# A decoder block on one core: two fetches at other times, and another order of the FFN's steps

## The chip, the cores and the metric

The kernel runs on one core of a Trainium2 chip, in one launch. The metric is the device time of that core in microseconds (us); shorter is better. Engines are named as the profile names them: PE multiplies matrices (PEld is its weight load), DVE and ACT work on vectors, POOL does very little here, SP only issues DMAs. Each engine works through its own instructions in the order of the program and waits for others by semaphores; the same holds for the queue of DMA issues on SP (SPq) and on ACT (ACTq).

## The reference

One layer of a decoder on 256 positions of width 2048, in float32. What matters here, cut down:

```python
a = rmsnorm(h, norm_mix_pre)
proj = a @ w_in                      # 17408 columns, split below
q_a, k_a, v_a, q_r, f_r, i_r, g_r, gate_a, gate_r = split_columns(proj)
attn  = dilated_window_attention(...)          # 8 heads, three groups of keys
r_out = hgrn2_chunked(...) * silu(g_r)         # gated recurrence, normalised
y = sigmoid(gate_a) * (attn @ w_attn_branch) + sigmoid(gate_r) * (r_out @ w_hgrn_branch)
h = h + rmsnorm(y @ w_mix_out, norm_mix_post)

a = rmsnorm(h, norm_ffn_pre)
gt, up = split(a @ w_ffn_gate_up)              # 2 x 5632 columns
ff = (silu(gt) * up) @ w_ffn_down
h = h + rmsnorm(ff, norm_ffn_post)
```

## The kernel before

Every weight is read once from DRAM into a `raw` tile. ACT rounds it to a shorter format (`hi`, or `w` in the profile), DVE subtracts that from the weight (`lo`, or `wl`), and PE makes three products for each pair of operands, high by high, high by low, low by high. A matmul takes 128 rows by 512 columns.

**Items.** The whole layer is a list of items that are run in order by the loop at the end. Two kinds are of interest. A *chunk* (in the middle of the layer: keys, queries, gates, branches) is 512 KB of weights; two chunks share a `raw` tile. A *step* (FFN gate and up, down product, mixing) is 1 MB: two rows of 128 by two groups of 512 columns. Before item i is multiplied, `prepare(i)` splits item i+2 (`AHEAD` is 2), fetches the presums of item i+4, and loads up to item i+5. There are three `raw` tiles, three `w` tiles and three `wl` tiles.

**Plain steps and steps by seven.** An order such as `GATE_UP4` lists pairs (m, kind): m is the pair of input rows, kind is 0 for a plain step of eight products in three parts (24 matmuls), and 1 or 2 for a step by seven, a Strassen-like scheme of seven products (21 matmuls). A step by seven multiplies sums of weights, so its split is longer. With kind 1 the sums are made on DVE in the split itself (`sum`, L432, L438, L439), then rounded by ACT (L437, L440, and L443 for the plain parts `dh`) and subtracted on DVE (L445, L447). With kind 2 the sums were made earlier by `weight_sums`, lie in DRAM as `presum`, and are fetched as `s` (L424 to L428 split them). The input sums that PE needs for it (`h7[m]`) come from `pair_sums`, a generator which runs a piece at a time in `lanes[1]`; lanes advance twice in a step.

**The FFN.** There are eleven blocks of 2 x 512 columns, eight steps each. Block 0 is plain; blocks 1 to 10 take the order `GATE_UP4`. Within a block the steps are counted from 0. Blocks use the two pools of four PSUM banks (`acc` and `aux`) in turn: the four plain sums of a block lie in one pool, and the three sums that only steps by seven write (`p5`, `p6`, `p7`) in the other, which is free again when the block before has been evacuated (`evac_ffn`, L1333). After step 1 of a block (`turn=1`) `turn_act` transposes the result of the block before on PE (L1302) into two banks of that other pool, ACT copies them out (L1303), and they go to DRAM (`acts`). So two of the four banks are held when step 2 begins with `p6`, `p5`, `p7`, in this order; `p7` needs the first that ACT has emptied. In the order of the program the split of step 3 stands before `turn_act`, since `prepare(1)` runs ahead of it.

**The start of the FFN's block 1.** `begin_wides` runs whatever is left in the lanes before block 1, with `flush(lanes[1])`: at that point the sums for m = 0 and 1 are made, those for m = 2 half way, those for m = 3 not begun.

**The down product.** It takes the activations back from DRAM: `fetch_act` issues `act<-acts` on SP, `prep_act` splits them (L572 on ACT, L576 on DVE) inside the split of a down step. The first two activations are asked for by a hook that the last FFN block runs after a step:

```python
wides[-3].post = lambda c: fetch_act(c // 2 - 2) if c in (4, 6) else None
```

The split of the first down step is in `prepare(6)` of that block. The first down block puts its plain sums in the same pool as the last FFN block.

**The gates.** The sigmoid gates of both branches were computed early and lie in DRAM (`waits`). Six of them (512 KB each) are fetched back by `fetch_gates`, all before the first of the 16 chunks that compute the last two gates; those chunks are followed by 16 chunks of the recurrent branch (`evac_rec_branch`, L1092, uses the first four gates) and 16 of the attention branch (L1102 uses the other two). All the while, `weight_sums` reads weights for the presums (`pre`, L299), adds them on DVE four chunks later (L307 to L311) and stores them.

Of the kernel before, what the change touches and what calls it, by code (L numbers as in the profile page):

```python
# [20 lines left out]
P = 128  # L21
# [19 lines left out]
    [(2, 0), (3, 0), (4, 0), (0, 1), (5, 0), (6, 0), (1, 1), (7, 0)],  # L41
    [(2, 0), (3, 0), (0, 1), (4, 0), (1, 1), (5, 0), (6, 0), (7, 0)],
]
GATE_UP4 = [(4, 0), (5, 0), (0, 2), (6, 0), (1, 1), (2, 2), (3, 1), (7, 0)]
PLACE = (0, 2, 1, 3)
DOWN = [[(m, m in by7) for m in range(KF // 2)] for by7 in (range(4, 20, 3), range(3, 19, 3))]

# [52 lines left out]
def tile_hybrid_block(ctx: ExitStack, tc: tile.TileContext, t, out):  # L100
# [13 lines left out]
    def nm(s):  # L114
        serial[0] += 1
        return f"{s}_{serial[0]}"

    def rslot(s):
        return rpool.tile([P, 1024], F32R, tag="r", bufs=16, name=nm(s))

    def hslot(s):
        return hpool.tile([P, 2, 512], F32, tag="h", bufs=4, name=nm(s))
# [77 lines left out]
    def fslot(s):  # L200
        return fp[0].tile([P, 1024], F32, tag="f", bufs=N_F, name=nm(s))
# [13 lines left out]
    blocks, chunks, wides, steps = [], [], [], []  # L215
    items_pre = {}
# [26 lines left out]
    def add_wide_block(*args, **kw):  # L243
        b = Wide(*args, **kw)
        wides.append(b)
        for i in range(len(b.order)):
            n = len(steps)
            slots.append(lambda n=n: load_wide(n))
            items.append((steps, n, len(slots) - 1))
            steps.append([b, i, None, None])  # L250
# [394 lines left out]
    evacs, turns, lanes, queue = deque(), deque(), [deque(), deque()], deque()  # L645
# [3 lines left out]
    def advance(q):  # L649
        if q:  # L650
            try:
                next(q[0])
            except StopIteration:
                q.popleft()
                return

    def flush(q):
        while q:
            advance(q)
# [192 lines left out]
    def nslot(s):  # L852
        return fslot(s).rearrange("p (b c) -> p b c", b=2)

    def fetch(dst, key, rows, **sizes):
        nc.sync.dma_start(dst, waits[key].rearrange(rows, **sizes))
# [3 lines left out]
            vN[half, g] = nslot("v")  # L860
            fetch(vN[half, g], ("v", g, half), "(j two) c -> j two c", two=2)

    def fetch_gates():
        for j in range(4):
            gates["r", j] = nslot("gate")
            fetch(gates["r", j], ("r", j), "(b p) c -> p b c", p=P)
        for j in range(2):
            gates["a", j] = hslot("gate")
            fetch(gates["a", j], ("a", j), "(b p) c -> p b c", p=P)

    qkT, vN = {}, {}

# [200 lines left out]
    gates = {}  # L1073
# [217 lines left out]
    act_t, h7 = [], {}  # L1291
# [19 lines left out]
    def fetch_act(upto):  # L1311
        while len(act_in) <= min(upto, 2 * len(act_t) - 1, KF // 2 - 1):
            x = rslot("act").bitcast(F32)
            nc.sync.dma_start(x, act_t[len(act_in) % (KF // 4)])
            act_in.append(x.rearrange("p (k t) -> p k t", k=4))
# [132 lines left out]
    def start_attention(half):  # L1448
        def go():
            queue.extend(attention(half, h) for h in range(4))  # L1450
        return go
# [5 lines left out]
    def begin_wides():  # L1457
        flush(lanes[0])
        flush(evacs)
        flush(lanes[1])  # L1460

    def more_y(c):
        if c == 3:
# [33 lines left out]
    for half in range(2):  # L1497
        for g in range(3):
            c = 1024 * g + 512 * half
            add_wide(w_in, KD, COL_Q + c, xT, evac_rope(("q", half, g), 0))  # L1500
            if g == 2:
                items_pre[len(chunks)] = lambda half=half: fetch_values(half)
            add_wide(w_in, KD, COL_K + c, xT, evac_rope(("k", half, g), 2,
                     start_attention(half) if g == 2 else None))
    items_pre[len(chunks)] = fetch_gates
    for j in range(2, 4):
        add("N", w_in, KD, COL_GA + 512 * j, xT, evac_gate(("a", j)))
    for j in range(4):
# [17 lines left out]
    for j in range(1, 11):  # L1526
        add_wide_block(w, (512 * j, FF + 512 * j), GATE_UP4, lambda k: hT[0](k),
                       lambda m: h7[m], evac_ffn, j % 2 == 0,
# [3 lines left out]
                       lambda m: a7[m], evac_down, j % 2 == 0, prep=prep_act,  # L1532
                       pre=begin_down if j == 0 else None, turn=3 if j == 0 else None)

    wides[-3].post = lambda c: fetch_act(c // 2 - 2) if c in (4, 6) else None
    back.append(
        weight_sums([n for n, (b, i, *_) in enumerate(steps) if b.order[i][1] == 2])
    )
# [13 lines left out]
    for i in range(len(items)):  # L1552
        kind, n, _ = items[i]
        b, c = kind[n][:2]
# [98 lines left out]
```

## Time and profile before

| | us |
|---|---|
| median of 3 runs | 1719.29 (1718.66 to 1719.31) |
| the profiled execution | 1719.58 |
| its span, first to last instruction | 1717.8 |
| PE busy | 1693.9 |
| DVE busy | 1438.2 |
| ACT busy | 915.8 |

The profiled execution is 0.29 us over the median. In lists of instructions the first column is the start (us from the first instruction), the second the time in us, then engine, line, operation, output and inputs, shapes and count; in brackets the idle time just before it on its engine and what ended it. A matmul shows about 0.39 us there, since it is pipelined; the next one starts much sooner.

### The profile page before, as it was taken

Reading aid. Unit: us, or ns where it says so; the run is one execution under the profiler, and the core shown is the slowest. Engines: PE = TensorE matmul, PEld = TensorE weight load, DVE = VectorE, ACT = ScalarE, POOL = GpSimd, SP = SyncE. Lnnn points to the kernel's source line nnn. Section 1 sums busy time; section 2 is a strip of 40 time slices with the busy share of each in tenths; the row PEclk is TensorE's granted clock in tenths of the full one; section 3 lists DMA queues with packets and bytes.
Section 4 is the critical chain, followed back from the end, with each engine's and each line's share of the span. In section 5 each row is a group of like instructions: output and inputs, shape, how many; then the busy total and the mean of one; then the engine's idle time right before and its main releaser. Section 6 shows DMA issues by size and latency. Waiting matters only on the chain.

```text
span 1717.8 us, 21815 instructions
## 1 busy us (share of the span) xinstructions
PE 1693.9 (99%) x8309; PEld 1422.9 (83%) x8309; DVE 1438.2 (84%) x1654; ACT 915.8 (53%) x1031; POOL 8.7 (1%) x17
## 2 busy tenths in 40 slices
PE   9999999999999999999999999999999999899997
PEld 7888888888888888888888877888888888688886
DVE  6998888867898998875568878988888888798998
ACT  6655555544434334445445556555555555565663
POOL 0000000000000000000000010000000000000000
PEclk9999999999999999999999999999999999999999
DMA  8567666678877776788457646777777777777773
GB/s 288 196 222 258 233 232 225 218 239 300 270 245 254 268 241 233 267 309 291 149 172 276 213 149 223 266 256 255 246 245 245 247 254 255 245 256 265 242 252 128
DMA packets 228905, 413.49 MB, mean 241 GB/s; under 512 B 12816, under 2 KB 79552, under 8 KB 226240
## 3 DMA queue, kind: packets, MB, share of 16 engines
q1 hardware_dynamic: 218544, 373.93, 64.7%
q10 hardware_dynamic: 10192, 38.15, 5.9%
q8 instruction: 65, 1.06, 0.2%
q14 instruction: 40, 0.33, 0.1%
q0 software_dynamic: 64, 0.02, 0.0%
HBM read 376.92 MB, written 35.13 MB: 240 GB/s over the span
## 4 chain that ended last, share of the span: by engine, by line
PE 91%; DVE 4%; DMA 2%; ACT 2%; issue 1%; SPq 0%; DVEq 0%; ACTq 0%
PE acc L137 57%; PE aux L137 32%; DMA pre<-in_w_ffn_gate_up 1%; DVE wl L418 1%; ACT w L416 1%; DMA s<-presum 0%; DMA gate<-waits 0%; DMA act<-acts 0%; PE aux L608 0%; PE aux L930 0%; DVE w L363 0%; PE aux L1302 0%; DVE fz L1429 0%; DVE dl L447 0%; PE acc L1302 0%
## 5 line engine op out<-in xcount | busy, mean ns | idle before, releaser
L137 PE MATMUL acc<-xT,w 128*128 128x256 f32 (+1 forms) x2048 | 367.1, 338 | 0.2 <-DVE w L363 0.2
L418 DVE TENSOR_TENSOR wl<-raw,w 128x2048 fp32r<-128x2048 f32 (+1 forms) x140 | 304.4, 2183 | 69.8 <-ACT w L416 68.0
L137 PEld LDWEIGHTS acc<-xT,w 128*128 128x128 f32 x2048 | 311.4, 188 | 44.9 <-DVE w L363 1.0
L362 ACT ACTIVATE w<-raw 128x1024 fp32r<-128x1024 f32 x176 | 185.9, 1058 | 245.9 <-PE acc L137 182.9
L416 ACT ACTIVATE w<-raw 128x2048 fp32r<-128x2048 f32 (+1 forms) x140 | 254.3, 1826 | 105.1 <-PE acc L137 36.2
L363 DVE TENSOR_TENSOR w<-raw,w 128x1024 fp32r<-128x1024 f32 x176 | 214.9, 1222 | 98.6 <-ACT w L362 98.1
L137 PE MATMUL acc<-w,xT 128*128 128x512 f32 x578 | 169.5, 392 | 2.3 <-DVE w L363 2.3
L437 ACT ACTIVATE w<-sum 128x1024 fp32r<-128x1024 f32 x57 | 60.5, 1062 | 179.8 <-DVE sum L432 172.6
L137 PE MATMUL acc<-w,hT 128*128 128x512 f32 x472 | 152.9, 392 | 0.5 <-DVE hT L619 0.5
L445 DVE TENSOR_TENSOR wl<-sum,w 128x1024 fp32r<-128x1024 f32 x114 | 137.2, 1221 | 13.0 <-ACT w L437 13.0
L137 PEld LDWEIGHTS acc<-w,xT 128*128 128x128 f32 x578 | 108.1, 188 | 24.7 <-DVE w L363 2.6
L137 PE MATMUL aux<-w,hT 128*128 128x512 f32 x360 | 115.7, 389 | 0.0
L447 DVE TENSOR_TENSOR dl<-raw,dh 128x1536 fp32r<-128x1536 f32 x57 | 100.2, 1757 | 14.4 <-ACT dh L443 13.1
L137 PE MATMUL aux<-w,xT 128*128 128x512 f32 x344 | 109.8, 389 | 0.0
L137 PEld LDWEIGHTS acc<-w,hT 128*128 128x128 f32 x472 | 88.4, 188 | 19.4 <-DVE hT L619 0.9
L137 PE MATMUL acc<-wl,hT 128*128 128x512 f32 x236 | 91.9, 389 | 0.0
L137 PE MATMUL acc<-w,a 128*128 128x512 f32 x268 | 84.9, 394 | 6.6 <-DVE e L1333 6.6
L443 ACT ACTIVATE dh<-raw 128x1536 fp32r<-128x1536 f32 x57 | 84.1, 1476 | 8.0 <-PE aux L137 4.4
L137 PE MATMUL aux<-w,a 128*128 128x512 f32 x268 | 83.6, 389 | 0.0
L137 PE MATMUL acc<-w,so 128*128 128x512 f32 x240 | 81.1, 391 | 1.2 <-ACT act L1303 1.2
L137 PEld LDWEIGHTS aux<-w,hT 128*128 128x128 f32 x360 | 67.6, 188 | 14.1
L137 PEld LDWEIGHTS aux<-w,xT 128*128 128x128 f32 x344 | 64.6, 188 | 13.3
(295 smaller groups left out, 2984.3 us busy)
## 6 DMA issues: line engine op xcount, KB each, us to landing
raw<-in_w_in SPq DMA_DIRECT2D x270, 512.0 KB, 4.8
raw<-in_w_ffn_gate_up SPq DMA_DIRECT2D x156, 512.0 KB, 4.8
raw<-in_w_ffn_down SPq DMA_DIRECT2D x88, 512.0 KB, 5.3
pre<-in_w_ffn_gate_up SPq DMA_DIRECT2D x40, 512.0 KB, 6.7
presum<-pre ACTq DMA_DIRECT2D x20, 1024.0 KB, 4.7
s<-presum SPq DMA_DIRECT2D x40, 512.0 KB, 7.0
raw<-in_w_mix_out SPq DMA_DIRECT2D x32, 512.0 KB, 4.9
act<-acts SPq DMA_DIRECT2D x22, 512.0 KB, 6.4
```

The lines of the kernel that those rows point to most:

```text
L137: nc.tensor.matmul(ps, lhsT, rhs, start=start, stop=stop, skip_group_check=True)
L362: nc.scalar.activation(wh, raw, AF.Copy)
L363: nc.vector.tensor_sub(wl, raw, wh.bitcast(F32))
L416: nc.scalar.activation(hi[:, c], raw[:, c], AF.Copy)
L418: nc.vector.tensor_sub(lo[:, c], raw[:, c], hi[:, c].bitcast(F32))
L437: nc.scalar.activation(hi[:, :1024], s[:, :1024], AF.Copy)
L443: nc.scalar.activation(dhi, d, AF.Copy)
L445: nc.vector.tensor_sub(lo[:, c], s[:, c], hi[:, c].bitcast(F32))
L447: nc.vector.tensor_sub(dlo, d, dhi.bitcast(F32))
```

## The change

Four edits. In `GATE_UP4` the fourth and fifth step change places: the steps by seven stood at places 2, 4, 5 and 6, and stand now at 2, 3, 5 and 6. `fetch_gates` is split into six fetches, one before each second chunk from the twelfth on. `begin_wides` no longer runs all sums in `lanes[1]`, but only until those of m = 1 are there; the others go on in the lanes. And the first two activations of the down product are asked for after steps 1 and 3 of the last FFN block, not after 4 and 6.

```diff
-GATE_UP4 = [(4, 0), (5, 0), (0, 2), (6, 0), (1, 1), (2, 2), (3, 1), (7, 0)]
+GATE_UP4 = [(4, 0), (5, 0), (0, 2), (1, 1), (6, 0), (2, 2), (3, 1), (7, 0)]
...
-    def fetch_gates():
-        for j in range(4):
-            gates["r", j] = nslot("gate")
-            fetch(gates["r", j], ("r", j), "(b p) c -> p b c", p=P)
-        for j in range(2):
-            gates["a", j] = hslot("gate")
-            fetch(gates["a", j], ("a", j), "(b p) c -> p b c", p=P)
+    def fetch_gate(key, slot):
+        def go():
+            gates[key] = slot("gate")
+            fetch(gates[key], key, "(b p) c -> p b c", p=P)
+        return go
...
     def begin_wides():
         flush(lanes[0])
         flush(evacs)
-        flush(lanes[1])
+        while 1 not in h7:
+            advance(lanes[1])
...
-    items_pre[len(chunks)] = fetch_gates
+    for j in range(6):
+        key, slot = (("r", j), nslot) if j < 4 else (("a", j - 4), hslot)
+        items_pre[len(chunks) + 12 + 2 * j] = fetch_gate(key, slot)
...
-    wides[-3].post = lambda c: fetch_act(c // 2 - 2) if c in (4, 6) else None
+    wides[-3].post = lambda c: fetch_act(c // 2) if c in (1, 3) else None
```

## The prediction

> **What bounds the kernel now.** The page first: how much of the span PE leaves unused.
>
> ```profile
> span 1717.8 us, 21815 instructions
> ...
> PE 1693.9 (99%) x8309; PEld 1422.9 (83%) x8309; DVE 1438.2 (84%) x1654; ACT 915.8 (53%) x1031; POOL 8.7 (1%) x17
> ```
>
> PE is the bound, and no edit removes a matmul. All that can move is its idle 23.9 us, and what is added to it. So next the waits of PE (us in total, times, longest):
>
> ```profile
> PE acc L137 <- DVE e L1333: 6.6, 1, 6.6
> PE acc L137 <- DVE w L363: 2.5, 2, 2.3
> PE acc L137 <- ACT act L1303: 1.2, 1, 1.2
> PE aux L137 <- DVE dl L447: 1.1, 1, 1.1
> ```
>
> These four lines are what the edits can touch: the first is at the start of the down product, the second among the gate chunks, the other two in FFN block 1. FFN blocks 2 to 10 have no wait of PE: there an edit of the order can only keep the time or add to it.
>
> **Edit 1, the activations.** Here are, from the instructions in order of time, the end of the last FFN block and the start of the down product, then two pieces of the chain that ended last, and one stretch of time (its length, PE, PEld, DVE, ACT and POOL busy, PE's granted clock, DMA share, GB/s).
>
> ```profile
> 1424.91 2.48 DVE L1333 TENSOR_TENSOR e<-aux,e 128x512 f32<-128x512 f32 x4
> ...
> 1448.15 8.74 SPq L285 DMA_DIRECT2D raw<-in_w_ffn_down  x4
> 1456.94 1.94 SPq L1314 DMA_DIRECT2D act<-acts  x1
> 1463.39 0.63 ACT L572 ACTIVATE a<-act 128x512 fp32r<-128x512 f32 x1 [7.40 <-DMA act<-acts]
> 1467.46 0.39 PE L137 MATMUL acc<-w,hT 128*128 128x512 f32 x1
> 1473.67 2.48 DVE L1333 TENSOR_TENSOR e<-acc,e 128x512 f32<-128x512 f32 x4
> 1474.50 0.77 PE L137 MATMUL acc<-w,a 128*128 128x512 f32 x1 [6.65 <-DVE e L1333]
> ```
>
> ```profile
> 1426.16 10.88 PE acc L137 x48
> 1474.50 23.69 PE acc L137 x96
> ```
>
> ```profile
> 1467.80:1500.00 32.20, 25.55 (x110) 21.10 (x110) 26.50 (x31) 16.61 (x17) 0.00 (x0) 0.89 0.74 250
> ```
>
> The fetch stood on SP behind two steps' weight loads, was issued at 1456.94 and had landed at 1463.39. ACT stood still 7.40 us in front of it, and behind L572 stood on ACT and DVE the splits of two down steps, the gathering of the sevens, and L1333, which empties the banks that the down product needs. PE's last matmul began at 1467.46, the next at 1474.50. At 10.88 / 48 = 0.227 us a matmul, that is 7.04 - 0.23 = 6.8 us lost.
>
> Then the chain: 96 matmuls took 23.69 us, at 0.227 they take 21.77, so 1.9 us more went at a lower clock (0.89 on the mean of that stretch). Together 8.7 us. The Trainium skill, "TensorE: Matmul & The Clock Gate", section "What's actually happening", says that after an idle window of about 3.4 us the array runs at half rate until it has been busy about as long. By that the loss would be some 1.7 us (an estimate from the page), the sum 8.5; the row, 1.9, is taken, and it agrees.
>
> What is late next, once the fetch is early? It now follows the load of step 6 on SP. That load waits for the split of step 3 to free its `raw` tile, which I put at about 1441 below, so the data lie there near 1448, some 8 us before the split of the first down step can start (1456). The second fetch comes before the load of the second down step. Neither moves behind a wait of its own: their two `act` slots were freed by the split of step 2 and by step 0 of this block. On SP the loads of steps 7 and of the first two down steps now stand behind a 512 KB fetch each, half a step's bytes.
>
> The new last link is L1333. In a regular block it starts 1.25 us before the next block's first matmul (1424.91 against 1426.16), and its first quarter (0.62 us) frees the first bank. The down block needs that one at once, because it takes the same pool, and the second bank six matmuls later (1.36 us). That cover holds by 0.6 us. Two L576 (0.7 us each) are new on DVE there against a regular block; the first falls into DVE's old idle time, the second while ACT rounds the weights. So I take the full 8.7; the ends are 0 (the fetch is hidden nowhere) and 8.7.
>
> **Edit 2, the gates.** The instructions, one piece of the chain, two stretches, and the lists for the tiles `pre` and `gate`:
>
> ```profile
> 760.39 3.96 SPq L856 DMA_DIRECT2D gate<-waits  x6
> 779.63 0.48 PE L137 MATMUL acc<-w,xT 128*128 128x512 f32 x1
> 779.79 0.69 DVE L307 TENSOR_TENSOR pre<-pre 128x512 f32<-128x512 f32 x1 [5.36 <-DMA pre<-in_w_ffn_gate_up]
> 782.40 2.79 PE L137 MATMUL acc<-w,xT 128*128 128x512 f32 x11 [2.29 <-DVE w L363]
> ```
>
> ```profile
> 768.40 11.31 DMA pre<-in_w_ffn_gate_up
> ```
>
> ```profile
> 760.00:785.00 25.00, 22.71 (x108) 18.81 (x107) 16.13 (x26) 8.73 (x11) 0.00 (x0) 1.00 0.92 319
> ...
> 805.00:825.00 20.00, 20.00 (x106) 17.18 (x105) 9.81 (x13) 12.31 (x15) 0.00 (x0) 1.00 0.65 212
> ```
>
> ```profile
> L299 SPq DMA_DIRECT2D pre<-in_w_ffn_gate_up x40: 367/469/1460, 357.6 to 792.8; - x40
> ...
> DMA to landing us min/median/max: 3.8/6.0/11.3
> ```
>
> ```profile
> L1092 DVE TENSOR_TENSOR part<-acc,gate x8: 683/684/686, 828.3 to 870.8; 128x512 f32<-128x512 f32 x8
> ```
>
> Six gates, 3 MB, go out at 760 in a stretch whose DMA share is 0.92. The weights for a presum behind them take 11.31 us to land (median 6.0). DVE stands 5.36 us in front of them with a split (L363) queued behind, and PE waits for that split: 782.40 - 779.63 - 0.23 = 2.5 us, and 0.1 more in the next 11 matmuls. At the median, 6.0 us, the weights land 5.3 us earlier, which is all of DVE's wait. So 2.6 us go; the ends are 0 and 2.6.
>
> What the moved fetches meet: the twelfth chunk is near 800, the last `pre` load went out at 792.8, and the DMA share there is 0.65. One gate on every second chunk (5.4 us of PE) adds 512 KB / 5.4 us, about 97 GB/s, to 212: 309, below the 319 shown. The first gate is used at 828.3, over 20 us after its fetch. Their slots were held by attention and the recurrence, which are further on by then; behind each fetch on SP stands one pair of weight loads, three pairs deep. I cost them at nothing.
>
> **Edit 3, the order, in blocks 2 to 10.** Rows of block 10, before:
>
> ```profile
> 1433.74 2.29 DVE L418 TENSOR_TENSOR wl<-raw,w 128x2048 fp32r<-128x2048 f32 x1
> ...
> 1437.52 1.09 ACT L1303 ACTIVATE act<-aux 128x512 f32<-128x512 f32 x2 [3.91 <-PE aux L1302]
> 1438.90 0.62 PE L137 MATMUL aux<-w,so 128*128 128x512 f32 x2
> 1439.97 1.05 ACT L440 ACTIVATE w<-sum 128x1024 fp32r<-128x1024 f32 x1
> 1440.92 1.47 ACT L443 ACTIVATE dh<-raw 128x1536 fp32r<-128x1536 f32 x1
> 1442.30 2.00 ACT L424 ACTIVATE w<-s 128x1024 fp32r<-128x1024 f32 x2
> 1448.04 1.22 DVE L432 TENSOR_TENSOR sum<-raw 128x1024 f32<-128x1024 f32 x1
> 1450.75 1.06 ACT L440 ACTIVATE w<-sum 128x1024 fp32r<-128x1024 f32 x1 [0.33 <-DVE sum L439]
> ```
>
> Before, step 3 is plain: its rounding on ACT needs nothing from DVE and is done when ACT reaches L1303 (it idles 3.91 us there, for PE). After, step 3 is a step by seven, and on ACT L437, L440 and L443 stand ahead of L1303, L440 waiting for DVE's sums. DVE comes to that split at 1433.74. From L432 to L440 takes 1450.75 - 1448.04 = 2.71, from L440 to L443 0.95, from there to the next instruction of ACT 1.38: L1303 starts at 1433.74 + 5.04 = 1438.78, not 1437.52. PE wants the emptied bank for `p7` at the second matmul of the 1438.90 row, 1439.13. Block 1 shows when it gets one, and edit 4 needs the same rows:
>
> ```profile
> 1060.68 0.40 PE L137 MATMUL acc<-w,so 128*128 128x512 f32 x1
> 1061.67 1.06 ACT L1303 ACTIVATE act<-acc 128x512 f32<-128x512 f32 x2
> 1062.30 0.50 PE L137 MATMUL acc<-w,so 128*128 128x512 f32 x1 [1.22 <-ACT act L1303]
> 1082.34 0.50 PE L137 MATMUL aux<-dl,hT 128*128 128x512 f32 x1 [1.14 <-DVE dl L447]
> ```
>
> ```profile
> 1050.00:1092.00 42.00, 39.64 (x178) 32.21 (x177) 39.81 (x42) 23.91 (x21) 0.00 (x0) 1.00 0.66 226
> ```
>
> There PE resumed 0.63 us after L1303's start. So `p7` gets its bank at 1439.41, 0.28 us late, in each of nine blocks. A wait costs a little more than it shows: 1062.30 - 1060.68 - 0.23 = 1.39 for the 1.22. I take 0.35 a block, 3.2 us in all. The ends are 0 (the margin is a few tenths of a sum of five durations) and 0.7 a block, 6.3.
>
> The gain that edit 3 could bring is that a third neighbouring step by seven no longer has to wait for the `dh`/`dl` tiles of the first; but PE waits for no split in these blocks, so it is worth nothing there. The split of step 3 ends on DVE near 1440.7, 1.6 us before PE wants it (1442.3); the later ones keep 2 us or more. Its `raw` tile is held until then and not until 1436, so the load of step 6 goes out nearly 5 us later, at 1441, for a split that starts at about 1448.5, with 6 us to land: covered.
>
> **Edit 4, the sums in two parts, with edit 3 in block 1.** DVE is busy 39.81 of 42 us here: it is the bound, and PE waited twice, 1.22 and 1.14 (1.4 and 1.3 with the restart). The flush held the split of step 2 back behind the sums of m = 2 and 3; now they come later, but all before steps 5 and 6. Nothing is taken off DVE. The wait at step 6 shrinks; that at `p7` grows, because L1303 now stands behind a step by seven there too. DVE reaches that split at about 1058.3 (the two products of block 0, the split of step 2 and half the sums of m = 2 come first); 5.04 + 0.63 later is 1064.0, 1.7 us after the 1062.30 of before. PE then comes to that place in step 6 at about 1082.7, where it resumed at 1082.34, and DVE is done with that split by then. 0.4 us is within what such a sum can tell: I take 0; the ends are a gain of 2.7 (both waits) and a loss of 1.7.
>
> **Sum.** 1719.58 - 8.7 - 2.6 + 3.2 + 0 = 1711.5 for the profiled execution; the median of the runs is 0.29 lower: 1711.2. This kernel tells 0.2% (3.4 us) from no change.
>
> **Rivals.**
>
> *No wait for `p7`* (0.17): L1303 comes 0.3 us sooner than summed. For it: the margin is that thin. Against: all five durations are rows of these blocks. Then 1711.2 - 3.2 = 1708.0.
>
> *The down product still starts late* (0.14): L1333 or the two splits ahead of it end after PE, because its banks are those of the block before. Against: the 0.6 us of cover. With 2 to 4 us of it left, and part of the slow clock, 1713 to 1715. A rule of the Trainium skill would lead there too: "DMA: Bandwidth & Descriptors", section "Anatomy of one DMA", says that a DMA's semaphore wait is waited out on the issuing sequencer, so a fetch without a free slot would hold the weight loads behind it. The trace agrees (the fetch at 1456.94 came out right behind two such loads).
>
> *Slower* (0.04): ACT's detour through DVE's sums costs far more, because DVE starts step 3's sums later than its split of step 3 now (weights landing late behind a `raw` tile held longer). Each 1 us of that is 9 us of PE. To be 0.2% slower it takes 11.3 + 3.4 = 14.7 over nine blocks, 1.63 a block, so DVE 1.3 us later than 1433.74. Nothing shows that: ACT and DVE had the same bytes there in time. Then 1723 and more.
>
> *The early fetches do nothing* (0.05): the gates merely delay other loads, or the activations land as late. Each alone leaves 1714 or 1719.9.
>
> **Chances.** The forecast 0.60. Faster by over 0.2% (below 1715.9): 0.60 + 0.17 + 0.12 and a little of the last, 0.90; within 0.2% 0.06; slower 0.04. The range from the first rival (1708.0) to the late start (1714.8) leaves out about 2 in 10.
>
> **What would show it.** After: PE's wait for L1333 gone, the clock 1.00 at the start of the down product, no wait of ACT for `act`; no wait of L307 or L363 near 780; new waits of PE on L1303, ten of them, some 0.1 to 0.4 us each and one near 2.8 in block 1; no wait for L447. Wrong would be: waits of PE for L1303 over 0.7 us each, or DVE's L1333 ending after PE's last matmul of block 10.

## The result

The changed kernel takes 1711.36 us (1711.0 to 1712.65) for 1718.84 (1717.51 to 1719.31) before: a ratio of 0.9958, 95% interval 0.9944 to 0.9973, which is 7.2 us (the medians are 7.5 apart). The forecast was 1711.2, 8.1 less than the 1719.29 that it started from. Its profiled execution took 1711.36 us, 8.2 less than the profiled one of before. On its page, the lines for the span and PE:

```profile
span 1709.5 us, 21818 instructions
...
PE 1692.8 (99%) x8309; PEld 1420.4 (83%) x8309; DVE 1440.1 (84%) x1654; ACT 915.6 (54%) x1031; POOL 8.7 (1%) x17
```

PE is idle for 16.7 us now, 23.9 before. Its waits in the changed kernel (us, times, longest):

```profile
PE acc L137 <- ACT act L1301: 2.8, 1, 2.8
...
PE acc L137 <- DVE hT L619: 0.5, 1, 0.5
```

The list of the weight load's waits (PEld) has two more lines for ACT's copies, ten waits in all, where before it had one of 1.7 us:

```profile
PEld acc L137 <- ACT act L1301: 5.5, 5, 3.3
PEld aux L137 <- ACT act L1301: 2.8, 5, 0.6
```

Lines after the edited functions are two lower here: L1301 is L1303 of before, L1331 is L1333. The waits for L1333 (6.6), L363 (2.5) and L447 (1.1) are gone. One has grown: PE in block 1 waits 2.8 us for ACT's copies, 1.2 before.

**The start of the down product**, in the changed kernel, in order of time:

```profile
1441.61 0.75 SPq L1312 DMA_DIRECT2D act<-acts  x1
1449.36 0.41 SPq L1312 DMA_DIRECT2D act<-acts  x1
1456.11 0.61 ACT L572 ACTIVATE a<-act 128x512 fp32r<-128x512 f32 x1
1466.95 2.48 DVE L1331 TENSOR_TENSOR e<-acc,e 128x512 f32<-128x512 f32 x4
1467.80 0.39 PE L137 MATMUL acc<-w,hT 128*128 128x512 f32 x1
1468.03 0.39 PE L137 MATMUL acc<-w,a 128*128 128x512 f32 x1
```

The chain there, and the stretch (length, PE, PEld, DVE, ACT, POOL busy, PE's granted clock, DMA share, GB/s):

```profile
1462.07 27.88 PE acc L137 x123
```

```profile
1463.00:1495.00 32.00, 32.00 (x147) 26.55 (x147) 26.02 (x30) 20.22 (x20) 0.00 (x0) 1.00 0.79 265
```

The fetch leaves 15 us earlier, ACT no longer waits before L572, and PE runs through at a clock of 1.00: 27.88 / 123 = 0.227 us a matmul across the boundary. The block's last matmul (1467.80) and the down product's first (1468.03) are 0.23 us apart.

**The gates.** A line of the list of the tile `pre` (how long its loads took to land) and one of `gate`, DVE's first sum of the presum that was late before, and a stretch:

```profile
DMA to landing us min/median/max: 4.1/6.1/10.1
```

```profile
L856 SPq DMA_DIRECT2D gate<-waits x6: 413/464/995, 796.7 to 828.6; - x6
```

```profile
773.30 0.68 DVE L307 TENSOR_TENSOR pre<-pre 128x512 f32<-128x512 f32 x1
```

```profile
800.00:810.00 10.00, 10.00 (x58) 8.68 (x57) 5.33 (x5) 5.21 (x6) 0.00 (x0) 1.00 0.99 340
```

L307 does not wait there any more. Right behind the first of the moved fetches, from 800 to 810, the DMA share is 0.99, and PE is still fully busy.

**Blocks 2 to 10.** ACT's copies in blocks 2 and 10, before and after, give the length of a block:

```profile
1103.97 1.09 ACT L1303 ACTIVATE act<-aux 128x512 f32<-128x512 f32 x2 [3.91 <-PE aux L1302]
```

```profile
1101.78 1.06 ACT L1301 ACTIVATE act<-aux 128x512 f32<-128x512 f32 x2
```

And block 10 after, around the copies:

```profile
1433.66 1.22 DVE L432 TENSOR_TENSOR sum<-raw 128x1024 f32<-128x1024 f32 x1
...
1436.37 1.06 ACT L440 ACTIVATE w<-sum 128x1024 fp32r<-128x1024 f32 x1 [0.30 <-DVE sum L439]
1437.33 1.47 ACT L443 ACTIVATE dh<-raw 128x1536 fp32r<-128x1536 f32 x1
1438.71 1.06 ACT L1301 ACTIVATE act<-aux 128x512 f32<-128x512 f32 x2
1438.82 1.01 PE L137 MATMUL aux<-w,so 128*128 128x512 f32 x2
1439.68 0.40 PE L137 MATMUL aux<-wl,so 128*128 128x512 f32 x1
1449.25 1.23 DVE L432 TENSOR_TENSOR sum<-raw 128x1024 f32<-128x1024 f32 x1 [0.89 <-DMA raw<-in_w_ffn_gate_up]
```

Eight blocks from 1103.97 to 1437.52 were 41.69 us each; from 1101.78 to 1438.71 they are 42.12. L1301 starts 5.05 us after L432, as summed (5.04). The two matmuls at 1438.82 take 1.01 us for the 0.62 of before: the second is `p7`'s first, held for its bank. It starts 0.3 us late. No wait of PE is listed for it, because most of that time hides inside the 0.39 us for which a pipelined matmul is shown. The nine short waits stand in the weight load's list above (with the one of block 1), and what they cost, 3.8 us, is read from the length of a block.

**The account**, by matmuls and transposes of PE that both traces have (start before, start after). Where the stretch with the gates begins (757.86, 756.82) the changed execution is already 1.0 us ahead, though the two kernels are the same up to there. At the first matmul of the mixing product that waits for L1102 (915.11, 911.48) it is 3.6 ahead, so the gates bring 2.6. At the transposes ahead of the copies in block 2 (1103.34, 1099.86) it is 3.5 ahead: block 1 costs 0.15. At those of block 10 (1436.88, 1436.80) it is 0.1 ahead, and one more wait for `p7` follows: blocks 2 to 10 cost 3.8. The last matmul (1708.13, 1699.90) is 8.2 ahead, so the start of the down product brings 8.6. These add up to the 8.2 by which the two profiled executions differ.

### The profile page after: what moved, and what is told of

It reads as the page before. It is cut to its first block, busy times and chain, and to the rows that moved or that the text cites. A ratio compares the mean times of both kernels' runs of the same rounds, so it can differ in the third digit from the quotient of the medians.

```text
span 1709.5 us, 21818 instructions
## 1 busy us (share of the span) xinstructions
PE 1692.8 (99%) x8309; PEld 1420.4 (83%) x8309; DVE 1440.1 (84%) x1654; ACT 915.6 (54%) x1031; POOL 8.7 (1%) x17
## 4 chain that ended last, share of the span: by engine, by line
PE 84%; DVE 7%; issue 5%; ACT 3%; DMA 1%; SPq 0%; DVEq 0%; ACTq 0%
PE acc L137 55%; PE aux L137 28%; ACT w L416 2%; DVE e L1331 1%; DVE wl L418 1%; DVE wl L425 1%; DVE e L1337 1%; DVE sum L432 1%; ACT w L424 1%; DMA pre<-in_w_ffn_gate_up 1%; DVE sum L439 0%; DVE sum L438 0%; PE aux L928 0%; ACT act L1301 0%; PE aux L608 0%
## 5 line engine op out<-in xcount | busy, mean ns | idle before, releaser
L418 DVE TENSOR_TENSOR wl<-raw,w 128x2048 fp32r<-128x2048 f32 (+1 forms) x140 | 305.3, 2184 | 88.0 <-ACT w L416 86.0
L363 DVE TENSOR_TENSOR w<-raw,w 128x1024 fp32r<-128x1024 f32 x176 | 214.9, 1222 | 102.5 <-ACT w L362 101.9
L447 DVE TENSOR_TENSOR dl<-raw,dh 128x1536 fp32r<-128x1536 f32 x57 | 100.1, 1757 | 6.8 <-ACT dh L443 3.4
L137 PE MATMUL aux<-w,so 128*128 128x512 f32 x222 | 76.2, 394 | 0.6
```

What stands on the lines that cost most here:

```text
L137: nc.tensor.matmul(ps, lhsT, rhs, start=start, stop=stop, skip_group_check=True)
L363: nc.vector.tensor_sub(wl, raw, wh.bitcast(F32))
L418: nc.vector.tensor_sub(lo[:, c], raw[:, c], hi[:, c].bitcast(F32))
L447: nc.vector.tensor_sub(dlo, d, dhi.bitcast(F32))
```

## The experiments

All ratios are against the kernel before, timed beside the run.

**Edit 1 alone.**

```diff
-    wides[-3].post = lambda c: fetch_act(c // 2 - 2) if c in (4, 6) else None
+    wides[-3].post = lambda c: fetch_act(c // 2) if c in (1, 3) else None
```

> The kernel before with edit 1 alone (both activations asked for after steps 1 and 3 of the last FFN block). Theory: PE's wait at the start of the down product (6.6 us) and the slow clock behind it (1.9 us) both go, 8.7 us less than before, and no wait of PE on L1333 is left. Rival (the down product starts late anyway, because L1333 or the two down splits are the next link): 4 to 6 us less, with a wait of 2 to 4 us left in front of the first down matmul.

1711.63 us for 1719.70; ratio 0.9950 (0.9938 to 0.9963), 8.1 us less. No wait for L1333 is left:

```profile
PE acc L137 <- DVE w L363: 2.4, 1, 2.4
PE aux L137 <- DVE dl L447: 1.3, 1, 1.3
PE acc L137 <- ACT act L1303: 1.3, 1, 1.3
```

The theory holds, and edit 1 alone gives as much as all four together: the other three sum to about nothing. In this execution the clock falls behind the wait of 2.4 us near 780, which costs 1.6 us more (last section).

**Edit 2 alone** (its last lines; `fetch_gates` is split as above).

```diff
...
-    items_pre[len(chunks)] = fetch_gates
+    for j in range(6):
+        key, slot = (("r", j), nslot) if j < 4 else (("a", j - 4), hslot)
+        items_pre[len(chunks) + 12 + 2 * j] = fetch_gate(key, slot)
```

> The kernel before with edit 2 alone (the gates fetched one by one from the twelfth chunk on). Theory: the weights for the presum land within about 6 to 7 us, DVE does not wait for them, PE's wait near 780 goes: 2.6 us less. Rival (the gates delay other loads where they are now): 0 to 2 us less, with a new wait of PE on L363 between 795 and 845.

1717.36 for 1719.70; ratio 0.9984 (0.9975 to 0.9993), 2.3 us less. The wait near 780 is gone, and no wait of PE appears between 780 and 845. The theory holds. PE's wait at the down product is 7.6 us in its trace (6.6 before), so part of the gain is given back there in this run.

**Edit 3 alone.**

```diff
-GATE_UP4 = [(4, 0), (5, 0), (0, 2), (6, 0), (1, 1), (2, 2), (3, 1), (7, 0)]
+GATE_UP4 = [(4, 0), (5, 0), (0, 2), (1, 1), (6, 0), (2, 2), (3, 1), (7, 0)]
```

> The kernel before with edit 3 alone (steps by seven at places 2, 3, 5, 6, all first sums still made ahead of block 1). Theory (ACT's copies of the transposed result stand behind the sums of step 3): blocks 2 to 10 last 42.1 us instead of 41.7, 3.8 us more; in block 1 DVE reaches step 3's sums at about 1061.8, so the bank for p7 comes at about 1067.5, a wait of some 6.4 us for 1.2 before, and after a wait this long the clock is low for a while (up to 1.9 us more); the wait at the down product shrinks by about 1 us: 6 to 9 us slower than before. Rival (the swap costs nothing, the blocks last longer after the change for another reason): within 1.5 us of before, blocks of 41.7 us.

1729.26 for 1719.70; ratio 1.0053 (1.0040 to 1.0065), 9.6 us more. Its waits of PE, and a stretch behind the one in block 1:

```profile
PE acc L137 <- ACT act L1303: 6.3, 1, 6.3
PE acc L137 <- DVE e L1333: 5.7, 1, 5.7
PE acc L137 <- DVE w L363: 2.9, 1, 2.9
```

```profile
1069.40:1073.00 3.60, 3.60 (x9) 2.88 (x10) 2.00 (x2) 2.98 (x3) 0.00 (x0) 0.53 0.91 320
```

The wait of 6.3 us was expected at 6.4, the smaller wait at the down product at 1 us less (5.7 for 6.6). The clock is 0.53 in the stretch behind the wait in block 1. Blocks 2 to 10 last 42.13 us (ACT's copies in blocks 2 and 10 at 1112.45 and 1449.51). The total is 0.6 over the top of what was expected: behind the wait for L363 (2.9 us here) the clock is low as well (0.61 from 782 to 785), which it was not in the profile of before. The rival falls: this edit costs time by itself.

**Edit 4 alone.**

```diff
-        flush(lanes[1])
+        while 1 not in h7:
+            advance(lanes[1])
```

> The kernel before with edit 4 alone (the sums of m = 2 and 3 left in the lanes). Theory: ACT's copies in block 1 no longer stand behind the sums, so PE's wait for p7 (1.2 us) goes; DVE is the bound of block 1 and is done with the split of step 6 at about 1080.3 to 1081, so a wait of 0.7 to 1.4 us stays there: 1.3 to 1.9 us less than before. Rival (as the prediction had it for edits 3 and 4 together, the wait only moves): within 0.5 us of before.

1717.60 for 1719.70; ratio 0.9987 (0.9978 to 0.9996), 2.1 us less. The wait for ACT's copies is gone and the one at step 6 is smaller:

```profile
PE aux L137 <- DVE dl L447: 0.8, 1, 0.8
```

That is the theory's place, and a little more than its size (1.3 to 1.9); part of the last tenths may be other waits of that execution (L363, 2.0 for 2.3).

**All but edit 3.**

```diff
-GATE_UP4 = [(4, 0), (5, 0), (0, 2), (1, 1), (6, 0), (2, 2), (3, 1), (7, 0)]
+GATE_UP4 = [(4, 0), (5, 0), (0, 2), (6, 0), (1, 1), (2, 2), (3, 1), (7, 0)]
```

> The changed kernel with edit 3 taken back (edits 1, 2 and 4 alone). Theory: blocks 2 to 10 last 41.7 us again, 3.8 us less than with all four edits, and in block 1 the wait for p7 (2.8 us) gives way to a wait of 0.8 us for the split of step 6, as in the run with edit 4 alone: 5 to 6 us less than with all four, 12.5 to 14.5 less than before. Rival (the order earns something at the ends of blocks or at the start of the down product that the sums do not show): no more than 3 us less than with all four, and a wait of PE near 1455 to 1465 that all four do not have.

1705.43 for 1719.35; ratio 0.9916 (0.9903 to 0.9930), 13.9 us less, and 5.9 less than all four edits. In its trace ACT's copies stand at 1098.21 and 1431.76 in blocks 2 and 10, 41.69 us a block; the only wait of PE over 0.5 us from block 1 of the FFN to the end of the down product is that of 0.8 us for step 6 of block 1. This is the fastest order of the steps found here, and it is the old one.

**All four, p7 asked for later.** The same matmuls in another order:

```diff
             prod("p5", sums(0), t, at[1], last)
+            if by7 == 2:
+                prod((1, 1), act_of(1, 1), t, at[3])
             prod("p7", sums(2), t, at[0], last)
-            prod((1, 1), act_of(1, 1), t, at[3])
+            if by7 != 2:
+                prod((1, 1), act_of(1, 1), t, at[3])
```

> The changed kernel, all four edits, with the three matmuls of p7 moved behind the three of the plain sum (1, 1) in the steps by seven whose sums come from DRAM; the same matmuls, p7's bank is asked for 0.68 us later. Theory (blocks 2 to 10 last 0.42 us longer because p7 waits for the bank that ACT empties): those blocks last 41.7 us again and block 1's wait falls from 2.8 to 2.1 us: 4.5 us less than with all four edits, about 12 less than before. Rival (neighbouring steps by seven slow PE or ACT in some other way, or the weights come later): blocks of 42.1 us, at most 0.7 us less.

1708.62 (1706.60 to 1710.28) for 1719.35; ratio 0.9934 (0.9921 to 0.9946). ACT's copies in blocks 2 and 10, and block 1's wait:

```profile
1103.23 1.06 ACT L1304 ACTIVATE act<-aux 128x512 f32<-128x512 f32 x2
...
1436.77 1.06 ACT L1304 ACTIVATE act<-aux 128x512 f32<-128x512 f32 x2
```

```profile
1060.81 0.50 PE L137 MATMUL acc<-w,so 128*128 128x512 f32 x1 [2.13 <-ACT act L1304]
```

```profile
1061.00:1064.00 3.00, 3.00 (x9) 2.37 (x9) 2.93 (x7) 2.40 (x3) 0.00 (x0) 0.59 0.78 251
```

A block lasts 41.69 us again, though ACT's copies still stand behind step 3's sums. That shows that the 0.42 us a block are `p7`'s wait for its bank and nothing else of the new order. The gain on the changed kernel is 2.7 us, not the 4.5 expected: behind the wait of 2.1 us the clock is at 0.59 in this execution.

**The gates in one burst, later** (its last lines; `fetch_gates` is whole again).

```diff
...
-    for j in range(6):
-        key, slot = (("r", j), nslot) if j < 4 else (("a", j - 4), hslot)
-        items_pre[len(chunks) + 12 + 2 * j] = fetch_gate(key, slot)
+    items_pre[len(chunks) + 12] = fetch_gates
```

> The changed kernel with all six gate fetches issued together, ahead of the twelfth chunk (3 MB at about 800 us, when the last weights for a presum are under way or landed). Theory (the gates hurt only by standing in front of the weights that DVE waits for, not by coming together): within 1 us of the changed kernel, no wait of PE on L363. Rival (the burst delays the weights of the chunks wherever it stands): 1.5 to 4 us more than the changed kernel, with a wait of PE between 805 and 825.

1713.40 for 1719.35; ratio 0.9963 (0.9950 to 0.9975). That is 2.0 us more than the changed kernel by the medians, which the theory had not (0.9 us by the two ratios, whose intervals overlap). But there is no wait on L363, and PE is busy throughout from 790 to 850. The difference lies in block 1. Here is the stretch behind the 2.82 us wait in this run, and then the same stretch of the changed kernel, whose wait has the same length:

```profile
1061.00:1064.00 3.00, 3.00 (x9) 2.30 (x8) 2.93 (x7) 2.49 (x3) 0.00 (x0) 0.54 0.81 251
```

```profile
1061.00:1064.00 3.00, 3.00 (x15) 2.46 (x14) 2.93 (x7) 2.70 (x3) 0.00 (x0) 1.00 0.85 259
```

Nine matmuls in 3 us for fifteen. ACT's copies of block 1 and block 2 are 43.67 us apart here and 42.14 in the changed kernel (1059.84 and 1103.51; 1059.64 and 1101.78); that is 1.5 of the 1.7 us by which the two profiled executions differ.

**The activations after steps 3 and 5.**

```diff
-    wides[-3].post = lambda c: fetch_act(c // 2) if c in (1, 3) else None
+    wides[-3].post = lambda c: fetch_act(c // 2 - 1) if c in (3, 5) else None
```

> The changed kernel with the two activations asked for after steps 3 and 5 of the last FFN block, not after 1 and 3. Theory (what the first fetch needs is to stand ahead of the load of the second down step on SP, which waits for the split of step 6): it is issued near 1446 to 1450 and lands before 1457, no wait of PE at the start of the down product, within 1 us of the changed kernel. Rival (the fetch needs the lead of several steps): a wait of 1 to 3 us there.

1713.47 for 1719.35; ratio 0.9963 (0.9950 to 0.9975), 2.1 us more than the changed kernel by the medians, with no wait of PE at the down product. In block 1 the clock is 0.54 in the same 3 us. So the same was tried without edit 3, where block 1 has no long wait.

**The burst, and the activations after steps 3 and 5, each without edit 3.** The two diffs above, and the old `GATE_UP4`.

> Edits 1, 2 and 4, with all six gate fetches together ahead of the twelfth chunk; block 1 has no long wait of PE here, so that its clock can't differ. Theory (the 2 us that the burst cost with all four edits came from a slow clock after the 2.8 us wait in block 1, not from the gates): within 0.6 us of the run with edits 1, 2 and 4 (1705.4), no wait of PE over 0.5 us among the chunks. Rival (the burst itself costs PE time): 1.5 to 2.5 us more than that run.

1705.65 for 1720.05; ratio 0.9914 (0.9900 to 0.9927).

> Edits 1, 2 and 4, with the two activations asked for after steps 3 and 5 of the last FFN block, not after 1 and 3. Theory (the same: the 2 us were the clock in block 1; the first fetch needs only to stand ahead of the second down step's load on SP): within 0.6 us of the run with edits 1, 2 and 4 (1705.4), no wait of PE at the start of the down product. Rival (the later fetch costs time at the start of the down product): 1.5 to 2.5 us more.

1705.90 for 1720.05; ratio 0.9914 (0.9900 to 0.9927). Both lie within 0.5 us of all but edit 3 (1705.43): the theory holds in both. Neither the burst nor the later fetch costs time by itself, and in the two profiled executions the 2 us were the clock in block 1; that it fell in the other executions of these two kernels too is argued from their times. The gates land late in the burst, as the list of their tile shows, and PE does not wait for them:

```profile
DMA to landing us min/median/max: 6.2/11.4/13.8
```

In the other run the first fetch goes out at 1444.14, and ACT uses it at 1450.96 without a wait. There it stood on SP behind the load of the first down step (1443.21) and ahead of that of the second (1451.07), and that is early enough.

## Why the prediction was right

**Edit 1: right in size and mechanism.** 8.7 us forecast, 8.6 in the account between the two traces, 8.1 at the medians alone. The fetch was put at about 1441 (1441.61). Of the 0.6 us of cover 0.46 was left: L1331 starts at 1466.95, its first quarter (0.62) ends at 1467.57, and the down product's first matmul starts at 1468.03. So the rival of a late start falls. One of the signs of being wrong was badly put: L1331 does end after PE's last matmul of block 10 (1469.43 against 1467.80), and nothing waits for it, because the banks are needed one by one.

**Edit 2: right.** 2.6 forecast, 2.6 in the account, 2.3 alone. That the fetches cost nothing where they stand now was right for another reason than the bandwidth that was summed up: the estimate of 309 GB/s was exceeded (340, share 0.99), and even the burst cost PE nothing. No DVE instruction between the chunks waits for that traffic once the presums are done; in the burst's run without edit 3 ACT stood still once for a branch's weights, 1.2 us, and PE did not. That the loads three pairs ahead hid it is argued. The presum's weights were put at the median landing time: they were there in time, and L307 has no wait.

**Edit 3, blocks 2 to 10: right, a little small.** 0.35 a block forecast, 0.42 measured, 3.8 us for 3.2. The sum of durations hit the start of the copies within 0.1 us; the term that was short was the restart behind the wait. So the rival of no wait for `p7` falls. Ten waits were forecast, and ten are there, but nine of them are listed for the weight load and not for PE, whose short gaps hide behind pipelined matmuls. Also short was the landing of step 6's weights: 6 us were allowed, DVE waited 0.89 us for them at 1449.25, within the 2 us that stood as cover.

**Edits 3 and 4 in block 1: right in sum, and the sum hid two parts.** Forecast 0, in the account 0.15; the wait for `p7` was put at 1.7 us later than before, and grew from 1.2 to 2.8. But edit 4 alone gains 2.1 us and edit 3 takes them back. The prediction said of both edits together that nothing is taken off DVE. Its work does stay the same, but with edit 4 by itself PE's wait for `p7` goes, and DVE loses no time to ACT on its way to the split of step 6. From the split that runs just ahead of the last flushed sums to the end of step 6's, DVE takes 33.67 us before (L418 at 1048.62, to 1082.29) and 31.80 with edit 4 alone (1046.60 to 1078.40). Before, it has 1.57 us of listed idle time in between, in five waits, all of them for ACT, and with edit 4 alone none. The longest of these waits:

```profile
1056.80 0.69 DVE L527 TENSOR_TENSOR so<-s,so 128x512 fp32r<-128x512 f32 x1 [0.77 <-ACT so L526]
```

**What was luck.** The profiled execution was forecast at 1711.5 and took 1711.36. That is closer than its terms: blocks 2 to 10 cost 0.6 us more than forecast, block 1 and edit 1 came out 0.3 worse together, and 1.0 us came from a stretch in which the two kernels are the same. Besides, the wait of 2.8 us in block 1 was not followed by a slow clock in this execution; in the two others with a wait of 2.82 us there it was, at a cost of 1.5 to 1.6 us.

**What it did not see.** A wait of 2 to 3 us can carry a slow clock behind it. In the profile of before it did not, behind the 2.29 us near 780, and the forecast counted it only for the 6.65 us wait. The Trainium skill, "TensorE: Matmul & The Clock Gate", section "What's actually happening", puts the fall at an idle window of about 3.4 us and says that the window runs free. The second agrees with the traces, where the clock changes only at marks 3.413 us apart (last section). As to the first, an idle time of 2.07 us between two marks was enough here, so the measurement decides.

## What to carry to other kernels

Two moved fetches and a piecewise flush bring 14 us; the reordered steps give 6 of them back, because a split that needs another engine now stands ahead of a copy that frees a bank. Before a step is moved, look on each in-order engine at what stands behind it, and at whose buffer that frees. Compare the length of a repeated block as well as the lists of waits: a loss of 0.4 us a block was in no list of PE's waits, only in the weight load's. And try the parts of a change alone, since here one part gave as much as all four.

## What the runs showed of the hardware

**PE's clock falls and rises at fixed marks.** In all twelve traces PE's granted clock is either 1.00 or 0.50 at any moment; a figure between them, as 0.54 or 0.61 above, is the mean of a stretch in which it changes. Every change lies a whole number of 3.413 us from the first one of its trace. With edit 3 alone, for example, it falls or rises at 782.68, 786.09, 1065.98, 1072.81, 1482.41 and 1489.23, which are 1, 82, 2, 120 and 2 times 3.413 us apart. (The times are those of the trace's record of the clock.) The kernel's waits do not move these marks, and their place differs from trace to trace: the first lies between 4.26 and 6.91 us. Here is edit 1 alone behind its wait, which ends at 781.25; PE works on at full speed for another 1.35 us, until a mark comes:

```profile
781.25:782.60 1.35, 1.35 (x6) 1.13 (x7) 1.31 (x3) 0.00 (x0) 0.00 (x0) 1.00 0.35 38
782.60:786.01 3.41, 3.41 (x10) 2.67 (x9) 2.29 (x2) 2.75 (x4) 0.00 (x0) 0.50 0.94 285
```

The next table cuts each wait of PE between 2 and 3 us at the marks of its own trace.

| run | PE idle (us) | before and after a mark | clock falls at |
|---|---|---|---|
| edit 4 alone | 2.03 | 0.91, 1.12 | does not fall |
| before | 2.29 | 1.62, 0.67 | does not fall |
| changed kernel | 2.82 | 1.64, 1.17 | does not fall |
| edit 1 alone | 2.37 | 0.30, 2.07 | 782.60 |
| `p7` asked for later | 2.13 | 2.13, no mark in it | 1061.56 |
| edit 3 alone | 2.94 | 2.53, 0.41 | 782.68 |
| activations after 3 and 5 | 2.82 | 0.23, 2.59 | 1061.27 |
| gates in one burst | 2.82 | 2.70, 0.12 | 1060.35 |

In these eight waits the length alone does not decide, but the longest idle time between two marks does: with 1.64 us or less the clock stayed, with 2.07 us or more it fell at the next mark. Between those two values nothing was measured. In the five that fell it was low for 3.41 us, and the 23 matmuls behind the wait with edit 1 alone took 7.14 us and not the 5.51 of before, 1.6 us more. Behind the waits of 5.7 us and more it fell in every trace too, and stayed low for two steps (6.83 us), part of it while PE still waited. It is a reason why two kernels with the same waits differ by 2 us.
